# Down projection finished one token tile at a time, and a one-tensor form for the attention factors

## The chip, the core and the metric

The kernel runs on one core of a Trainium2 chip. The metric is device time in microseconds for one execution of the whole program, a two-layer transformer block over 1024 image tokens and 256 context tokens. The names of the engines: PE is TensorE (matmul; PEld is its weight load), DVE is VectorE, ACT is ScalarE, POOL is GpSimd, and SP issues most of the DMAs.

## The reference

Both layers are computed for `h` (1024 tokens of 1024 features); layer 0 also updates the context. What the change touches are the differential attention of layer 1 and the down projections of both feed-forward blocks:

```python
def diff_attention(q, k, v, lam):
    scale = DIFF_DH ** -0.5
    def blk(qb):
        s = jnp.einsum('bqhmd,bkhmd->bhmqk', qb, k).astype(jnp.float32) * scale
        p = jax.nn.softmax(s, axis=-1)
        w = (p[:, :, 0] - lam * p[:, :, 1]).astype(v.dtype)
        return jnp.einsum('bhqk,bkhe->bqhe', w, v)
...
def conv_ffn(u, w_up, conv_w, conv_b, w_down):
    a, g = jnp.split(u @ w_up, 2, axis=-1)
    g = dwconv(g, conv_w, conv_b, FFN_PAD)
    return (jax.nn.gelu(g) * a) @ w_down
...
h = h + ga2 * conv_ffn(u, ffn_w_up[li], ffn_conv_w[li], ffn_conv_b[li], ffn_w_down[li])
```

The hidden width is 2816 = 22 x 128. There are 8 heads, each with two maps (`m` = 0, 1) that are softmaxed apart and subtracted with the factor `lam`.

## The kernel before

**Products.** Every fp32 product is made of three matmuls on a high and a low part of each operand (`mm3`, lines 116, 117 and 118). A high part is a rounded copy (line 283 on ACT, line 90 on POOL), a low part is the difference of the value and its high part (line 98, on DVE or POOL).

**Down projection** (`ffn_down`). Layer 0 has three rounds of token tiles (0 to 3, 4 to 6, 7 to 9), layer 1 two (0 to 3, 4 to 7). A token tile is 128 tokens; its sum `acc` fills two PSUM banks, and a round of four tiles fills all eight. In a round the 22 weight tiles (`f`, 128 x 1024) go by in order, each with the matching piece of the hidden layer: an *item* of the list `items`. Step `i` issues the loads of item `i + 3` (SP), the split of item `i + 1` into high and low parts (ACT, then DVE), then item `i`'s matmuls for all tiles of the round, six for a tile. The split weights lie in rings of four buffers (`wh`, `wl`), the split hidden pieces in rings of three (`hh`, `hl`), the raw weights in a ring of three (`wr`). From round 1 of layer 0 on a step also takes one piece of `extra`, which prepares the finished tiles for layer 1 (square and scale, turn on PE, split).

After the 22 items each tile of the round is evacuated: DVE multiplies `acc` by a gain into `dtmp` (line 1244), POOL adds that to `ht` (line 1245), SP writes the sum out (line 1246). The very last tile is done in two halves, both operations on DVE. All of this stands in a written order: an engine takes its instructions in the order of the code.

**After layer 0's last round** comes `layer1_front`, whose order a scheduler makes. Its first weights `w_in_c` use the same rings `wr`, `wh` and `wl`; POOL makes the high part (line 90) and DVE the low part (line 98).

**Differential attention** (`diff_attn`). A head has four pairs of token tiles `a` and `b`, 32 pairs in all. `ORDER1` lists the operations of one step and by how many steps each lags. For DVE a step is, in this order: `m1a`, `m1b` (row maximum of map 1, line 1471), `ra` (reciprocal, line 1481), `ta` (the factor `tt` = first sum x -lam x reciprocal, line 1485), `pa` (the two maps combined, line 1487), `rb`, `m0b`, `m0a`, `tb`, `pb`. ACT makes the exponentials (line 1477) and copies of the turned maps (1499, 1506). POOL does `ha`, `la`, `hb`, `lb`: the high part of a turned map (line 90, `wh<-wf`) and its low part (line 98, `wl<-wf`). PE does the scores (1466), the turning (1492) and the product with `v` (1447).

Of the kernel before, what the change touches and what calls it, by code (L numbers as in the profile page):

```python
# [12 lines left out]
F32R = mybir.dt.float32r  # L13
# [5 lines left out]
P = 128  # L19
# [40 lines left out]
class K:  # L60
# [1108 lines left out]
    def ffn_down(self, l, rounds, dst, chunks, after):  # L1169

        nc, io = self.nc, self.io
        with ExitStack() as st:
            F = self.sb(st, f"down{l}")
            extra = []
            if after:
                Un = self.sb(after, "u1cols", side="right")
                self.u = {}
                AB = self.mod_finish(1, 0, 0)
            items = [(r, f) for r in range(len(rounds)) for f in range(NF)]
            raws, parts = {}, {}  # L1180

            def fetch(i):
                r, f = items[i]
                w = self.W.tile([P, 1024], F32, tag="wr", bufs=NWR, name="wr")
                nc.sync.dma_start(w, io["ffn_down"][l, f * P:(f + 1) * P, :])
                n = len(rounds[r]) * P
                x = F.tile([P, 512], F32, tag="hr", bufs=4, name="hr")[:, :n]
                nc.sync.dma_start(x, self.hid_d[f, :, rounds[r][0] * P:rounds[r][0] * P + n])
                raws[i] = w, x

            def split(i):
                w, x = raws.pop(i)
                n = x.shape[-1]
                hs = [F.tile([P, 512], F32R, tag="h" + y, bufs=3, name="h" + y)[:, :n] for y in "hl"]
                self.split(x, *hs)
                parts[i] = hs, self.split_new(w)

            def columns(t, ht):
                u = self.u[t] = [Un.tile([P, KT, P], F32R, tag=f"u{x}{t}", name="u") for x in "hl"]
                xn = F.tile([P, D], F32, tag="xn", bufs=2, name="xn")  # L1200
                v = F.tile([P, KT, P], F32, tag="v", bufs=2, name="v")
                return [lambda: self.scaled(F, ht, xn, xn.rearrange("p (k c) -> p k c", c=P)),
                        lambda: self.turned(xn, AB, v), lambda: self.split(v, *u)]

            with self.tc.manual_schedule():
                parts[0] = self.ahead
                for i in range(1, 3):
                    fetch(i)
                for r, tiles in enumerate(rounds):
                    with ExitStack() as s2:  # L1210
                        PS = self.PS = self.ps(s2, f"psD{l}{r}")
                        self.twos = 4 - len(tiles)
                        acc = {t: PS.tile([P, 2, 512], F32, tag="acc", bufs=len(tiles), name="acc") for t in tiles}
                        hts = {}
                        if r == 1:
                            extra = [step for ch in chunks for step in self.mod_steps(F, 1, ch, 1)] + extra
                        for f in range(NF):
                            i = r * NF + f
                            if i + 3 < len(items):
                                fetch(i + 3)  # L1220
                            if i == 4:
                                gas = [self.ga(F, l, 1, c, f"ga{c}") for c in range(2 if l == 0 else 1)]
                            if f == 8:
                                for t in tiles:
                                    hts[t] = F.tile([P, D], F32, tag="ht", bufs=8, name="ht")
                                    nc.sync.dma_start(hts[t], self.hm_d[t])
                            if i + 1 < len(items):
                                split(i + 1)
                            hs, w = parts.pop(i)
                            for j, t in enumerate(tiles):  # L1230
                                for b in range(2):
                                    self.mm3(acc[t][:, b, :], [x[:, j * P:(j + 1) * P] for x in hs],
                                             [x[:, b * 512:(b + 1) * 512] for x in w], f == 0, f == NF - 1)
                            if r:
                                coming = sum(3 * len(x) for x in rounds[r:-1]) if after else 0
                                for _ in range(-(-(len(extra) + coming) // (len(items) - i))):
                                    if extra:
                                        extra.pop(0)()
                        for t in tiles:
                            tmp = F.tile([P, D], F32, tag="dtmp", bufs=4, name="dtmp")  # L1240

                            last = l == 1 and t == NTX - 1
                            for c in [slice(0, 512), slice(512, D)] if last else [slice(0, D)]:
                                nc.vector.tensor_mul(tmp[:, c], acc[t].rearrange("p a b -> p (a b)")[:, c], gas[t >= NTX][:, c])  # L1244
                                (nc.vector if last else nc.gpsimd).tensor_tensor(hts[t][:, c], hts[t][:, c], tmp[:, c], op=ADD)  # L1245
                                nc.sync.dma_start(dst(t)[:, c], hts[t][:, c])
                        if after and r + 1 < len(rounds):
                            for t in tiles:
                                extra += columns(t, hts[t])
                assert not extra  # L1250
# [171 lines left out]
    def diff_attn(self):  # L1422
        nc, tc = self.nc, self.tc
        with ExitStack() as st:
# [12 lines left out]
            def emit(op, p):  # L1437
# [30 lines left out]
                elif op[0] == "m":  # L1468
                    m = int(op[1])
                    Y["m", m] = A.tile([P, 1], F32, tag=f"m{m}", bufs=4, name="m")  # L1470
                    nc.vector.tensor_reduce(Y["m", m], Y["S", m][:, :TOK], axis=AX.X, op=ALU.max, negate=True)  # L1471
                elif op[0] == "e":
                    m = int(op[1])
                    Y["p", m] = A.tile([P, TOK], F32, tag=f"p{m}", bufs=3 - m, name="p")
                    if m:
                        Y["s"] = A.tile([P, 1], F32, tag="s", bufs=4, name="s")
                    nc.scalar.activation(Y["p", m], Y["S", m][:, :TOK], AF.Exp, bias=Y["m", m],  # L1477
                                         accum_out=Y["s"] if m else s0[:, h, t:t + 1])
                elif op[0] == "r":
                    Y["r"] = A.tile([P, 1], F32, tag="r", bufs=4, name="r")  # L1480
                    nc.vector.reciprocal(Y["r"], Y["s"])
                elif op[0] == "t":

                    Y["tt"] = A.tile([P, 1], F32, tag="tt", bufs=4, name="tt")
                    nc.vector.scalar_tensor_tensor(Y["tt"], s0[:, h, t:t + 1], self.nlam, Y["r"], op0=MUL, op1=MUL)
                elif op[0] == "p":
                    nc.vector.scalar_tensor_tensor(Y["p", 0], Y["p", 1], Y["tt"], Y["p", 0], op0=MUL, op1=ADD)  # L1487
                elif op[0] == "T":
                    g = int(op[1])
                    Y["T", g] = PS.tile([P, 512], F32, tag="tp", bufs=2, name="tp")  # L1490
                    for k in range(min(4, NT - 4 * g)):
                        nc.tensor.transpose(Y["T", g][:, k * P:(k + 1) * P],
                                            Y["p", 0][:, (4 * g + k) * P:(4 * g + k + 1) * P], self.ident)
                elif op[0] == "f":
                    g = int(op[1])
                    n = min(4, NT - 4 * g)
                    if "wf" not in Y:
                        Y["wf"] = A.tile([P, NT, P], F32, tag="wf", bufs=2, name="wf")
                    nc.scalar.copy(Y["wf"][:, 4 * g:4 * g + n], Y["T", g][:, :n * P].rearrange("p (k c) -> p k c", c=P))
                elif op[0] == "h":  # L1500
                    if i == 0:
                        for w in ("wh", "wl"):
                            X[w] = A.tile([P, NT, 256], F32R, tag=w, bufs=2, name=w)
                    self.round_to("p", X["wh"][:, :8, c], Y["wf"][:, :8])
                elif op[0] == "x":
                    nc.scalar.copy(X["wh"][:, 8:, c], Y["wf"][:, 8:])  # L1506
                else:
                    self.rest("p", X["wl"][:, :, c], Y["wf"], X["wh"][:, :, c])
# [224 lines left out]
```

## Time and profile before

| what | value |
|---|---|
| median of 3 runs | 3381.88 us (3379.8 to 3381.99) |
| the profiled execution's own time | 3376.81 us |
| its span | 3375.0 us |
| mean granted TensorE clock | 0.982 |
| PE busy over the span | 94% |
| DVE busy over the span | 70% |
| POOL busy over the span | 28% |
| DMA read / written | 319.89 / 111.34 MB |

A duration in the profile holds what an instruction waits for once it has been started, so one and the same instruction can have several durations; the gap ahead of it is what it waited for before that, and the square bracket of a row says whose work ended that gap. Shares over the whole span hide that the stages have different limits.

### The profile page before, as it was taken

To read this page: it belongs to the slowest core of one execution; us is meant where nothing else is said; L and a number is where in the kernel's file an instruction comes from. 1 tells how busy PE (TensorE), PEld (TensorE's weight loads), DVE (VectorE), ACT (ScalarE), POOL (GpSimd) and SP (SyncE) were. 2 spreads that over 40 slices of the span, in tenths; PEclk is the share of its full clock that TensorE was granted. 3 is DMA by queue.
4 is the path that set the end of the run, shared out by engine and by line. 5 is a ranking of instruction groups with operands and counts; after the bars stand their busy time and mean duration, and the time that the engine had idled before them with its cause. 6 is when DMAs were issued, how large, how long until landed. Compare 5 with 4: busy or idle time off the path is not lost.

```text
span 3375.0 us, 43426 instructions
## 1 busy us (share of the span) xinstructions
PE 3161.4 (94%) x16262; PEld 2615.9 (78%) x16262; DVE 2368.7 (70%) x3381; ACT 1411.5 (42%) x2444; POOL 951.7 (28%) x654
## 2 busy tenths in 40 slices
PE   8998989989799999999999999888888899999998
PEld 4777778878688888877777777677877678888887
DVE  6478978864877777544556896699997787666443
ACT  3355766743433333323342121577763433333222
POOL 2223578864000000001113332377774200000010
PEclk9999999999999999999999999999999999999999
DMA  7223954334132232154555555534414123222553
GB/s 265 71 76 127 285 145 104 90 115 144 60 104 99 87 106 92 65 195 148 195 183 210 146 165 163 142 99 114 130 44 169 57 99 105 77 87 79 194 189 119
DMA packets 232298, 434.07 MB, mean 129 GB/s; under 512 B 21484, under 2 KB 147692, under 8 KB 230296
## 3 DMA queue, kind: packets, MB, share of 16 engines
q1 hardware_dynamic: 230216, 424.49, 39.8%
q10 hardware_dynamic: 1872, 6.82, 0.6%
q8 instruction: 128, 2.10, 0.3%
q14 instruction: 82, 0.67, 0.1%
HBM read 319.89 MB, written 111.34 MB: 128 GB/s over the span
## 4 chain that ended last, share of the span: by engine, by line
PE 56%; DVE 13%; issue 5%; ACT 2%; DMA 2%; POOL 1%; SPq 0%; DVEq 0%; ACTq 0%; POOLq 0%
PE pB L116 5%; PE pB L118 5%; PE pB L117 5%; PE acc L118 4%; PE acc L116 4%; PE acc L117 4%; DVE m L1471 3%; PE pj L116 3%; DVE p L1487 2%; PE pj L117 2%; PE pj L118 2%; PE pE L118 2%; PE pE L116 2%; PE pE L117 2%; PE S L1466 2%
## 5 line engine op out<-in xcount | busy, mean ns | idle before, releaser
L98 DVE TENSOR_TENSOR wl<-wr,wh 128x1024 fp32r<-128x1024 f32 (+2 forms) x287 | 350.8, 1231 | 100.0 <-ACT wh L283 70.6
L118 PE MATMUL acc<-wl,hh 128*128 128x512 f32 x776 | 304.8, 393 | 7.7 <-DVE wl L98 7.6
L116 PE MATMUL acc<-wh,hh 128*128 128x512 f32 x776 | 305.4, 394 | 5.8 <-ACT wh L283 5.8
L1245 POOL TENSOR_TENSOR ht<-ht,dtmp 128x1024 f32<-128x1024 f32 x17 | 44.7, 2660 | 919.2 <-DVE dtmp L1244 919.2
L117 PE MATMUL acc<-wh,hl 128*128 128x512 f32 x776 | 303.7, 391 | 0.0
L98 POOL TENSOR_TENSOR wl<-wf,wh 128x1280 fp32r<-128x1280 f32 x64 | 221.7, 3465 | 106.1 <-ACT wh L1506 103.6
L1466 PE MATMUL S<-k,q 128*128 128x512 f32 (+1 forms) x768 | 197.6, 382 | 56.9 <-ACT p L1477 55.5
L283 ACT CAST wh<-wr 128x1024 fp32r<-128x1024 f32 (+1 forms) x223 | 222.0, 1006 | 66.1 <-DVE wr L999 42.2
L98 DVE TENSOR_TENSOR hl<-hr,hh 128x512 fp32r<-128x512 f32 (+1 forms) x108 | 74.5, 690 | 224.8 <-ACT hh L283 224.7
L116 PE MATMUL pB<-ht,wh 128*128 128x512 f32 x528 | 210.0, 398 | 15.2 <-ACT ht L283 4.8
L118 PE MATMUL pB<-lt,wh 128*128 128x512 f32 x528 | 209.7, 397 | 3.0 <-DVE lt L98 2.9
L117 PE MATMUL pB<-ht,wl 128*128 128x512 f32 x528 | 209.3, 396 | 0.8 <-DVE wl L98 0.8
L116 PE MATMUL pj<-wh,u 128*128 128x512 f32 x448 | 180.7, 403 | 17.8 <-DVE qT L98 14.5
L1477 ACT ACTIVATE p<-S,m 128x1280 f32<-128x1280 f32 x128 | 170.9, 1335 | 61.5 <-DVE m L1471 58.2
L1471 DVE TENSOR_REDUCE m<-S 128x1 f32<-128x1280 f32 x128 | 187.1, 1480 | 8.4 <-PE S L1466 7.6
L1466 PEld LDWEIGHTS S<-k,q 128*128 128x128 f32 x768 | 124.7, 193 | 78.2 <-ACT p L1477 64.1
L283 ACT CAST hh<-hr 128x512 fp32r<-128x512 f32 (+1 forms) x108 | 62.5, 579 | 290.0 <-PE acc L118 258.7
L118 PEld LDWEIGHTS acc<-wl,hh 128*128 128x128 f32 x776 | 146.6, 189 | 43.1 <-DVE wl L98 12.8
L117 PE MATMUL pj<-wh,u 128*128 128x512 f32 x448 | 178.8, 399 | 0.0
L118 PE MATMUL pj<-wl,u 128*128 128x512 f32 x448 | 178.0, 398 | 0.0
L1037 ACT COPY g<-pB 128x512 f32<-128x512 f32 x84 | 49.6, 590 | 304.9 <-PE pB L118 304.9
L116 PEld LDWEIGHTS acc<-wh,hh 128*128 128x128 f32 x776 | 146.7, 189 | 38.8 <-ACT wh L283 9.1
(420 smaller groups left out, 9093.8 us busy)
## 6 DMA issues: line engine op xcount, KB each, us to landing
wr<-ffn_down SPq DMA_DIRECT2D x110, 512.0 KB
wr<-ffn_up SPq DMA_DIRECT2D x90, 512.0 KB
wr<-w_mod SPq DMA_DIRECT2D x76, 512.0 KB
hid<-gc SPq DMA_DIRECT2D x44, 512.0 KB
k<-dk SPq DMA_DIRECT2D x14, 1280.0 KB
hr<-hid SPq DMA_DIRECT2D x64, 256.0 KB
wr<-w_in_c SPq DMA_DIRECT2D x24, 512.0 KB
mr<-w_mod SPq DMA_DIRECT2D x20, 512.0 KB
```

Of the source, the lines that this page charges most:

```text
L98: e.tensor_tensor(out, x, hi.bitcast(F32), op=SUB)
L116: mm(out, a[0], b[0], start=start, stop=False, skip_group_check=onto)
L117: mm(out, a[1], b[0], start=False, stop=False, skip_group_check=onto)
L118: mm(out, a[0], b[1], start=False, stop=stop, skip_group_check=onto)
L283: self.nc.scalar.copy(hi, x)
L1037: nc.scalar.copy(out, x)
L1245: (nc.vector if last else nc.gpsimd).tensor_tensor(hts[t][:, c], hts[t][:, c], tmp[:, c], op=ADD)
L1466: nc.tensor.matmul(Y["S", m][:, c0:c0 + n], heads[h]["q"][m][:, t * P:(t + 1) * P], heads[h]["k"][x, m, j], start=(x == 0), stop=(x == 1))
L1471: nc.vector.tensor_reduce(Y["m", m], Y["S", m][:, :TOK], axis=AX.X, op=ALU.max, negate=True)
L1477: nc.scalar.activation(Y["p", m], Y["S", m][:, :TOK], AF.Exp, bias=Y["m", m], accum_out=Y["s"] if m else s0[:, h, t:t + 1])
L1487: nc.vector.scalar_tensor_tensor(Y["p", 0], Y["p", 1], Y["tt"], Y["p", 0], op0=MUL, op1=ADD)
```

## The change

In `ffn_down` the steps of a round's last three items still load and split, but issue no matmul. After the last step each tile of the round takes the matmuls of these three items (18 of them), and is evacuated behind them, before the next tile's 18 are issued. For this the rings `hh` and `hl` get a fourth buffer, the three items' parts are kept until the round's end, and the pieces of `extra` are spread over three steps fewer. In the attention the factor `tt` is computed by a `tensor_scalar` with one tensor operand and two per-partition factors; before it was a `scalar_tensor_tensor` with two tensor operands and one factor.

```diff
+            ends = 3
...
-                hs = [F.tile([P, 512], F32R, tag="h" + y, bufs=3, name="h" + y)[:, :n] for y in "hl"]
+                hs = [F.tile([P, 512], F32R, tag="h" + y, bufs=4, name="h" + y)[:, :n] for y in "hl"]
...
+            def product(out, i, j):
+                hs, w = parts[i]
+                f = items[i][1]
+                for b in range(2):
+                    self.mm3(out[:, b, :], [x[:, j * P:(j + 1) * P] for x in hs],
+                             [x[:, b * 512:(b + 1) * 512] for x in w], f == 0, f == NF - 1)
...
-                            hs, w = parts.pop(i)
+                            if f >= NF - ends:
+                                continue
                             for j, t in enumerate(tiles):
-                                for b in range(2):
-                                    self.mm3(acc[t][:, b, :], [x[:, j * P:(j + 1) * P] for x in hs],
-                                             [x[:, b * 512:(b + 1) * 512] for x in w], f == 0, f == NF - 1)
+                                product(acc[t], i, j)
+                            parts.pop(i)
                             if r:
...
-                                for _ in range(-(-(len(extra) + coming) // (len(items) - i))):
+                                for _ in range(-(-(len(extra) + coming) // max(1, len(items) - i - ends))):
...
-                        for t in tiles:
+                        for j, t in enumerate(tiles):
+                            for e in range(i - ends + 1, i + 1):
+                                product(acc[t], e, j)
                             tmp = F.tile([P, D], F32, tag="dtmp", bufs=4, name="dtmp")
...
+                        for e in range(i - ends + 1, i + 1):
+                            parts.pop(e)
...
-                    nc.vector.scalar_tensor_tensor(Y["tt"], s0[:, h, t:t + 1], self.nlam, Y["r"], op0=MUL, op1=MUL)
+                    nc.vector.tensor_scalar(Y["tt"], s0[:, h, t:t + 1], self.nlam, Y["r"], op0=MUL, op1=MUL)
```

On PE, in round 0 of layer 0, this is how the first of the last three items is left before the change; `acc_13462` and `acc_13463` are the sums of tiles 0 and 1, `wh_14134` and `wl_14135` that item's weights:

```order
L117 MATMUL acc_13462<-wh_14134,hl_14131 128x512
L118 MATMUL acc_13462<-wl_14135,hh_14130 128x512
L116 MATMUL acc_13463<-wh_14134,hh_14130 128x512
L117 MATMUL acc_13463<-wh_14134,hl_14131 128x512
L118 MATMUL acc_13463<-wl_14135,hh_14130 128x512
```

And at the same place now; `wh_14170` and `wl_14171` are the next item's weights:

```order
L117 MATMUL acc_13462<-wh_14134,hl_14131 128x512
L118 MATMUL acc_13462<-wl_14135,hh_14130 128x512
L116 MATMUL acc_13462<-wh_14170,hh_14166 128x512
L117 MATMUL acc_13462<-wh_14170,hl_14167 128x512
L118 MATMUL acc_13462<-wl_14171,hh_14166 128x512
```

Where PE went on to the next tile with the same weights, it now stays on the tile and goes on to the next weights; the number of matmuls is the same.

On POOL, at the end of layer 0's last round, before (`wh<-wr` is the high part of a `w_in_c` tile, `ht<-ht,dtmp` the evacuation's addition):

```order
L260 TENSOR_SCALAR xn<-ht,rs_y 128x1024
L90 TENSOR_SCALAR wh<-wr 128x1024 x3
L1245 TENSOR_TENSOR ht<-ht,dtmp 128x1024
L90 TENSOR_SCALAR wh<-wr 128x1024
L1245 TENSOR_TENSOR ht<-ht,dtmp 128x1024 x2
```

And now:

```order
L260 TENSOR_SCALAR xn<-ht,rs_y 128x1024
L90 TENSOR_SCALAR wh<-wr 128x1024
L1256 TENSOR_TENSOR ht<-ht,dtmp 128x1024
L90 TENSOR_SCALAR wh<-wr 128x1024
L1256 TENSOR_TENSOR ht<-ht,dtmp 128x1024
L90 TENSOR_SCALAR wh<-wr 128x1024 x2
L1256 TENSOR_TENSOR ht<-ht,dtmp 128x1024
```

The roundings of the new stage's weights moved in between the additions. In the attention no row changes its place on any engine; on DVE the row of `tt` changes its kind, from `SCALAR_TENSOR_TENSOR` to `TENSOR_SCALAR`.

## Rows read from the trace of the kernel before

**Rows 1.** Two stretches: us; busy of PE, PEld, DVE, ACT, POOL; clock; DMA; GB/s

```profile
2143.00:2538.00 395.00, 339.85 (x2258) 300.91 (x2258) 379.29 (x322) 292.81 (x530) 279.81 (x126) 0.98 0.39 105
...
3129.00:3366.00 237.00, 235.91 (x1038) 194.71 (x1038) 93.82 (x92) 64.78 (x82) 14.20 (x6) 1.00 0.47 161
```

**Rows 2.** The factor `tt` by tile: duration in ns, least, median, greatest

```profile
L1485 DVE SCALAR_TENSOR_TENSOR tt<-s,nlam,r x64: 210/724/1501, 2143.2 to 2535.8; 128x1 f32<-128x1 f32 x64
```

**Rows 3.** The same, grouped over the attention: busy us, mean ns

```profile
L1485 DVE SCALAR_TENSOR_TENSOR tt<-s,nlam,r 128x1 f32<-128x1 f32 x64 | 66.1, 1033 | 3.3 <-ACT p L1477 1.5
```

**Rows 4.** Timeline of DVE over one pair: start, us, instruction

```profile
2298.79 2.88 DVE L1471 TENSOR_REDUCE m<-S 128x1 f32<-128x1280 f32 x2
...
2301.95 0.70 DVE L1485 SCALAR_TENSOR_TENSOR tt<-s,nlam,r 128x1 f32<-128x1 f32 x1
2302.69 1.55 DVE L1487 SCALAR_TENSOR_TENSOR p<-p,tt 128x1280 f32<-128x1280 f32 x1
...
2307.25 1.49 DVE L1485 SCALAR_TENSOR_TENSOR tt<-s,nlam,r 128x1 f32<-128x1 f32 x1
2308.77 2.30 DVE L1487 SCALAR_TENSOR_TENSOR p<-p,tt 128x1280 f32<-128x1280 f32 x1
2311.00 1.48 DVE L1471 TENSOR_REDUCE m<-S 128x1 f32<-128x1280 f32 x1
```

**Rows 5.** Timeline of POOL beside it

```profile
2301.60 1.05 POOL L90 TENSOR_SCALAR wh<-wf 128x1024 fp32r<-128x1024 f32 x1
2305.77 2.95 POOL L98 TENSOR_TENSOR wl<-wf,wh 128x1280 fp32r<-128x1280 f32 x1 [3.12 <-ACT wh L1506]
2308.69 1.04 POOL L90 TENSOR_SCALAR wh<-wf 128x1024 fp32r<-128x1024 f32 x1
2309.82 4.04 POOL L98 TENSOR_TENSOR wl<-wf,wh 128x1280 fp32r<-128x1280 f32 x1
```

**Rows 6.** Timeline of ACT, the pair's first exponential

```profile
2300.30 1.33 ACT L1477 ACTIVATE p<-S,m 128x1280 f32<-128x1280 f32 x1 [1.51 <-DVE m L1471]
```

**Rows 7.** A 128x1 instruction with one tensor operand, by line

```profile
L258 DVE TENSOR_SCALAR ss<-ss x38: 140/152/156, 6.6 to 2673.9; 128x1 f32<-128x1 f32 x38
```

**Rows 8.** Timeline of DVE at the end of layer 0's round 0

```profile
1563.29 5.30 DVE L1244 TENSOR_TENSOR dtmp<-acc,ga 128x1024 f32<-128x1024 f32 x4 [4.07 <-PE acc L118]
1568.51 1.28 DVE L98 TENSOR_TENSOR hl<-hr,hh 128x384 fp32r<-128x384 f32 x1
1569.72 3.40 DVE L98 TENSOR_TENSOR wl<-wr,wh 128x1024 fp32r<-128x1024 f32 x1
1573.04 0.14 DVE L258 TENSOR_SCALAR ss<-ss 128x1 f32<-128x1 f32 x1
```

**Rows 9.** Timeline of POOL beside it

```profile
1564.60 10.77 POOL L1245 TENSOR_TENSOR ht<-ht,dtmp 128x1024 f32<-128x1024 f32 x4 [286.50 <-DVE dtmp L1244]
```

**Rows 10.** Timeline of PE behind it

```profile
1573.17 0.50 PE L118 MATMUL acc<-wl,hh 128*128 128x512 f32 x1 [1.31 <-DVE wl L98]
...
1579.22 0.98 PE L270 MATMUL ntp<-ident,xn 128*128 128x128 f32 x7 [2.12 <-POOL xn L260]
```

**Rows 11.** The page's group of the low parts made on DVE

```profile
L98 DVE TENSOR_TENSOR wl<-wr,wh 128x1024 fp32r<-128x1024 f32 (+2 forms) x287 | 350.8, 1231 | 100.0 <-ACT wh L283 70.6
```

**Rows 12.** Timeline of PE behind layer 0's round 1

```profile
1677.32 0.51 PE L118 MATMUL acc<-wl,hh 128*128 128x512 f32 x1 [2.63 <-DVE wl L98]
```

**Rows 13.** Busy time and granted clock just behind it, columns as in rows 1

```profile
1677.00:1681.00 4.00, 3.68 (x9) 2.90 (x10) 2.58 (x8) 0.00 (x0) 2.62 (x2) 0.58 1.00 322
```

**Rows 14.** Timeline of DVE at the program's end

```profile
3361.41 4.77 DVE L1244 TENSOR_TENSOR dtmp<-acc,ga 128x1024 f32<-128x1024 f32 x4 [9.48 <-PE acc L118]
3366.21 1.76 DVE L1245 TENSOR_TENSOR ht<-ht,dtmp 128x512 f32<-128x512 f32 x1
...
3368.61 2.11 DVE L1245 TENSOR_TENSOR ht<-ht,dtmp 128x512 f32<-128x512 f32 x1
```

**Rows 15.** Timeline of POOL beside it

```profile
3362.71 7.46 POOL L1245 TENSOR_TENSOR ht<-ht,dtmp 128x1024 f32<-128x1024 f32 x3 [109.25 <-DVE dtmp L1244]
```

## The prediction

> **What bounds the kernel now.** I read the table of stretches first, since the page's 94% for PE is a mean over stages with different limits. In layer 1's down projection (3129 to 3366) PE is busy 235.91 of 237 us; in the attention (2143 to 2538) it is busy 339.85 of 395 while DVE is busy 379.29, that is 96% [rows 1]. So the attention is DVE's stage, and the down projections are PE's except at the ends of their rounds. In DVE's stage one group stands out: `tt`, one element per partition, has 64 instructions that together take 66.1 us, 1033 ns each [rows 3], though the quickest needs 210 ns [rows 2].
>
> The timelines of DVE and POOL laid side by side say why [rows 4, 5]. The first `tt` of the pair ends at 2302.65, and so does POOL's `wh` (2301.60 + 1.05). The second runs from 2307.25 to 2308.74; POOL's `wl` ends at 2308.72. The `p` behind it starts at 2308.77, while POOL's next `wh` runs to 2309.73, and ends 1.34 us after that, at 2311.07; the other `p`, with nothing beside it, takes 1.55. POOL suffers in turn: its second `wl` takes 4.04, and 2311.07 to its end at 2313.86 is 2.79. So a DVE instruction with two SBUF tensors and a POOL instruction exclude each other for a whole instruction, and where POOL has its next one ready, the DVE instruction that already waits goes first. The first goes for `hl` and `wl` behind a round as well: `wl` takes 3.40 beside POOL's additions [rows 8, 9] and 1.23 on average [rows 11]. An instruction with one tensor operand of 128x1 is not shut out: at 1573.04 one takes 0.14 in the middle of an addition [rows 8, 9], and none of 38 takes over 156 ns [rows 7].
>
> **The attention, step by step.** The new `tt` has one tensor operand of 128x1. Its two factors come by partition, which rows 7 don't show; its cost lies between 0.14 and the 1033 of now, and I take 0.2, nearest to rows 7 and to the quickest old one. That alone doesn't give 0.83 us back 64 times, because `p` right behind it has two SBUF tensors and meets the same POOL instruction. So I replay a pair.
>
> - First `tt`: it ends at about 2302.15 in place of 2302.65, but `p` then waits for POOL's `wh` to 2302.65 and ends 1.34 later at 2303.99, against 2304.24. That moves `m` of map 0, behind it, up by 0.25, and the second `tt`, but not POOL's `wl` beside that, which starts on ACT's release [rows 5]. Gain at the pair's end: 0.
> - Second `tt`: it is done by about 2307.5, and `p` waits for `wl` to end at 2308.72. It has then been waiting in the place that `tt` held, so it goes ahead of POOL's `wh`: 2308.72 + 1.34 = 2310.06, against 2311.07. Gain: 1.01.
> - What is late next: POOL's `wh` starts at 2310.06 and ends at 2311.10, its `wl` (2.95) at 2314.05. The next pair's `m` now starts 1.01 earlier, at 2309.99, so `wl` ends 4.06 into that pair, later than the 2.81 of now (2301.60 - 2298.79). The first `p`, asking at 3.4, waits for that and ends at 5.40; today it ends at 5.45. Nothing behind it moves.
>
> The pair shrinks from 12.21 us (2311.00 - 2298.79) to 11.20. The loop that then sets it is `m`, ACT's exponential, which starts on it [rows 6], ACT's copies, POOL's `wl`, which starts on them [rows 5], `p`, and `m`. PE needs 339.85/395 of 12.34 (a 32nd of the stretch), 10.6 us, so it still fits. How many pairs gain: 32 first factors of about 0.71 are 22.7 of the 66.1 us, and the 43.4 left are 29 of 1.49. Term: 29 x 1.01 = 29.3 us.
>
> The Trainium skill weighs in here. Its page "SBUF — State Buffer", section "SBUF: two separate sides", says that VectorE and GpSimd share a port pair as an exclusive lock for a whole instruction, and that VectorE needs it with two SBUF inputs or in a two-port performance mode. The page "VectorE: DVE Perf Modes", section "Mode 2×_2P — use both read ports for one tensor", gives that mode to fp32 `tensor_scalar`. Rows 4 and 5 agree with the lock. By the mode the new `tt` would be shut out like the old one and the term would be 0; the 0.14 at 1573.04 speaks against that for a single element per partition. It is the third rival below.
>
> **The ends of the rounds.** The matmul count is unchanged. PE issues one per 0.227 us (235.91/1038 [rows 1]), so a tile's 18 take 4.09 and a tile's six 1.36: before, the tiles of a round end 1.36 apart, now 4.09 apart. An addition on POOL takes 2.69 (10.77/4 [rows 9]), a multiplication on DVE about 1.3 (5.30/4 [rows 8]). Before, POOL fell behind and its additions covered the next split on DVE; now all but the last are over when PE leaves the round (T).
>
> - Behind the last tile: the multiplication ends at T + 1.4; the next item's `hl` (0.5) either slips in ahead of the addition or waits for it; `wl` ends at the latest 1.2 behind the addition, T + 1.4 + 0.5 + 2.5 + 1.1, about T + 5.5, and without any collision at T + 3.1. The new order adds one wait: this split needs buffers that three held items free only in the last tile, at T - 2.7, which is before DVE can take it.
> - Rounds 0 to 1 and 1 to 2 of layer 0: the next item lasts 18 x 0.227 = 4.1, so `wl` is wanted at about T + 4.4: a wait of 0 to 1.1, I take 1.1, since the collision is what rows 8 show. Before, 1.31 and, for the turning behind POOL's queue, 2.12 [rows 10]; the second goes, as POOL's additions are over. Gain 3.4 - 1.1 = 2.3, at most 3.4. At the second place 2.63 [rows 12], and behind it the clock fell to 0.58, between its levels of 1.2 and 2.4 GHz [rows 13], which costs 0.42 x 4 = 1.7. A wait of 1.1 is less than half of 2.63, and I let it cost no clock. Gain 4.3 - 1.1 = 3.2, at most 4.3.
> - Layer 1's round 0 has four tiles in the next item (5.4 us): covered, 0; without that cover 0.8.
> - Into `layer1_front`: three of four weight buffers are held to T - 2.7, T - 1.4 and T, so POOL's roundings stand between the additions. POOL: rounding to T - 1.7, addition to T + 1.0, two roundings to T + 3.1, addition to T + 5.8. DVE's low parts queue behind these, and the last ends at about T + 8. Loss between 0 and 1.5; I take 0.7.
> - The program's end: the last two DVE additions took 1.76 and 2.11 beside POOL's additions, which ran to 3370.17 [rows 14, 15]. Now POOL is done by T + 0.1. Nearest row for a free 128x512 addition: 0.14 + half of 1.23, about 0.7. So 1.06 + 1.41 = 2.5 earlier; the last write has fewer bytes in front of it, 0 to 1. I take 2.9.
>
> Sum: 2.3 + 3.2 - 0.7 + 2.9 = 7.7.
>
> The fourth buffer of `hh` and `hl` adds no instruction; what hides it is that a split already ran two items ahead of PE, and in layer 1's rounds PE waited for none (1.1 us of idle in 237 [rows 1]).
>
> **Total.** 29.3 + 7.7 = 37. The profiled execution took 3376.8, so 3339.8. The median of the runs, 3381.9, is 5.1 above it; on that footing I forecast 3345.
>
> **Rivals.**
>
> 1. The wait only moves to `p`: at the end of POOL's `wl` its next instruction gets in first. For it: the second `p` lost just so, to a `wh` that had already started. Against: both times DVE was waiting at an end, it won, with the second `tt` at 2308.74 and `p` at 2309.73. Then the attention gains 0, total -7.7: 3374.
> 2. More than forecast: ACT's copies come earlier in the shorter pair and PE becomes the bound. Its 10.6 with some of its present waits left, say the middle between that and 11.2, is 10.9, so 29 x 1.3 = 38; with the upper ends of the other terms (3.4 + 4.3 + 0 + 3.5 = 11.2) -49: 3333. For it: POOL still has slack. Against: `wl` follows ACT, and ACT follows `m`.
> 3. The change doesn't do what it says: the new `tt` is shut out as well. Attention 0, 3374.
> 4. Slower: the next split is shut out twice, `hl` by the last addition and `wl` by POOL's next instruction, so that `wl` comes at T + 6.6. At three ends PE then idles 2.2 and runs on at the slow clock (1.7): 3 x 3.9 = 11.7 against 7.7 now (3.4 + 4.3), and 0.9 in layer 1: +4.9, and with nothing from the attention 3387. It decides from the point at which POOL has a second instruction ready when the addition ends. Against: rows 8 show `hl` in between two additions.
>
> **How the numbers follow.** Forecast 0.70, with its own range of 3336 to 3354 (pairs 0.85 to 1.1 each, ends 5 to 11). Rival 1 has 0.13, rival 2 0.07, rival 3 0.06, rival 4 0.04. A measurement of this kernel tells about 0.2% from no change, 6.8 us. Forecast and rival 2 are faster by more, rivals 1 and 3 (7.7 us, 0.23%) in about half of the cases: 0.77 + 0.10 = 0.87 faster; the other half and most of rival 4 within, 0.11; slower 0.02. The range takes in rival 2 down to 3330, and rivals 1 and 3 up to 3374.
>
> **What would show it.** In the new profile: all `tt` at about 0.2; both `p` of a pair above 1.55, the second ending 1.3 after POOL's `wl`; `m` to `m` 11.2; POOL's second `wl` back to 2.95; DVE idle ahead of neither. At the round ends no wait of PE over 1.3 and no clock below full; the two last additions 0.7 each. I am wrong if `tt` still follows POOL's ends, if the second `p` ends behind POOL's `wh`, or if the pair stays at 12.2.

## The result and the profile after

The changed kernel takes 3339.66 us in the median of four runs (3337.66 to 3341.32); beside it the kernel before took 3380.84 (3379.58 to 3381.99). The ratio is 0.9878, with an interval of [0.9861, 0.9895], so it is 41 us faster, between 35 and 47. The forecast was 3345, with a range of 3330 to 3374. The profiled execution took 3341.32 with a span of 3339.5, which is 35.5 less than the span of before. Where these 35.5 lie is read by taking the same matmul in both traces and subtracting its start:

| stretch | forecast | read from the two traces |
|---|---|---|
| start, up to layer 0's down projection | 0 | 2.5 longer |
| layer 0, end of round 0 | -2.3 | -2.7 |
| layer 0, end of round 1 | -3.2 | -3.4 |
| last round's end and `layer1_front` | +0.7 | -1.2 |
| attention and what follows it, up to layer 1's feed-forward block | -29.3 | -26.4 |
| layer 1, end of round 0 | 0 | -0.4 |
| the program's end | -2.9 | -3.9 |

The 2.5 at the start lies in code that the change doesn't touch, almost all of it within the first 45 us. At 45 us the twelve other kernels profiled in this study are 1.5 to 3.0 us later than the one profiled execution of before as well, so it is that execution which was early there. At the start of the down projection they are 0.1 to 7.0 later, so a row of one trace on code that is the same may be off by some us. Without the 2.5 the sum is 38.0, against a forecast of 37.

In the table of stretches, the attention of the new profile is the first line (us; busy us and count of PE, PEld, DVE, ACT, POOL; clock; DMA share; GB/s); the second is the 4 us behind layer 0's round 1, which answer to [rows 13]:

```profile
2138.20:2507.10 368.90, 340.80 (x2264) 302.29 (x2265) 347.66 (x322) 293.39 (x531) 320.87 (x127) 0.97 0.42 112
1673.50:1677.50 4.00, 3.42 (x16) 2.50 (x15) 3.23 (x8) 0.00 (x0) 1.81 (x3) 1.00 0.69 219
```

PE's busy time in the attention is within 1 us of what it was [rows 1], in a stretch that is 26 us shorter; DVE is still busy for 94% of it. The clock behind the round is now 1.00, where it had been 0.58 [rows 13].

By tile and by group (as [rows 2, 3]), `tt` and the `p` behind it:

```profile
L1498 DVE TENSOR_SCALAR tt<-s,nlam,r x64: 268/274/278, 2138.4 to 2503.7; 128x1 f32<-128x1 f32 x64
L1500 DVE SCALAR_TENSOR_TENSOR p<-p,tt 128x1280 f32<-128x1280 f32 x64 | 138.2, 2160 | 2.2
L1498 DVE TENSOR_SCALAR tt<-s,nlam,r 128x1 f32<-128x1 f32 x64 | 17.5, 274 | 3.5 <-ACT p L1490 1.5
```

None of the 64 is shut out any more: 59 of them lie wholly inside a POOL instruction, and the slowest takes 278 ns. They gave up 66.1 - 17.5 = 48.6 us of DVE's busy time. Some 15 of these came back in `p`, whose mean rose from 1929 to 2160 ns. That is the wait which the prediction moved from `tt` to `p`. Timelines of DVE and of POOL over one pair (as [rows 4, 5]):

```profile
2291.34 0.27 DVE L1498 TENSOR_SCALAR tt<-s,nlam,r 128x1 f32<-128x1 f32 x1
2291.65 2.51 DVE L1500 SCALAR_TENSOR_TENSOR p<-p,tt 128x1280 f32<-128x1280 f32 x1
2294.09 2.88 DVE L1484 TENSOR_REDUCE m<-S 128x1 f32<-128x1280 f32 x2
...
2297.26 0.27 DVE L1498 TENSOR_SCALAR tt<-s,nlam,r 128x1 f32<-128x1 f32 x1
2297.57 1.90 DVE L1500 SCALAR_TENSOR_TENSOR p<-p,tt 128x1280 f32<-128x1280 f32 x1
```

```profile
2289.87 2.95 POOL L98 TENSOR_TENSOR wl<-wf,wh 128x1280 fp32r<-128x1280 f32 x1 [0.71 <-ACT wh L1519]
2292.79 2.28 POOL L90 TENSOR_SCALAR wh<-wf 128x1024 fp32r<-128x1024 f32 x1
2295.16 2.95 POOL L98 TENSOR_TENSOR wl<-wf,wh 128x1280 fp32r<-128x1280 f32 x1
2298.07 2.30 POOL L90 TENSOR_SCALAR wh<-wf 128x1024 fp32r<-128x1024 f32 x1
```

The second `p` (2291.65) waits until POOL's `wl` ends at 2292.82, and ends 1.34 us after that, at 2294.16. POOL's next instruction, `wh`, was started at 2292.79 but takes 2.28 in place of 1.04: it was the one that had to wait. So DVE's waiting instruction got the turn, twice in a pair, and POOL pays in `wh` what it paid before in its second `wl` (4.04 then, 2.95 now). From one second `p` to the next the pair takes 11.2 us. In the whole attention 58 of the 64 `p` end in this way, 1.3 us behind a `wl`.

At the end of layer 0's round 0, DVE, POOL and PE (as [rows 8, 9, 10]):

```profile
1569.90 1.23 DVE L1255 TENSOR_TENSOR dtmp<-acc,ga 128x1024 f32<-128x1024 f32 x1 [2.85 <-PE acc L118]
1571.04 0.55 DVE L98 TENSOR_TENSOR hl<-hr,hh 128x384 fp32r<-128x384 f32 x1
1571.50 3.42 DVE L98 TENSOR_TENSOR wl<-wr,wh 128x1024 fp32r<-128x1024 f32 x1
```

```profile
1571.20 2.63 POOL L1256 TENSOR_TENSOR ht<-ht,dtmp 128x1024 f32<-128x1024 f32 x1 [1.67 <-DVE dtmp L1255]
```

```profile
1574.97 0.50 PE L118 MATMUL acc<-wl,hh 128*128 128x512 f32 x1 [0.58 <-DVE ss L258]
```

PE leaves the round at T, just ahead of the last multiplication at 1569.90. `hl` slips in ahead of POOL's last addition, `wl` is shut out until that ends at 1573.83, and is done at T + 5.0. PE waits 0.58, and there is no second wait for the turning; the end of round 1 is the same to 0.1 us. At the program's end both halves' additions on DVE now take 0.69 (as [rows 14]):

```profile
3334.65 0.69 DVE L1256 TENSOR_TENSOR ht<-ht,dtmp 128x512 f32<-128x512 f32 x1
...
3335.98 0.69 DVE L1256 TENSOR_TENSOR ht<-ht,dtmp 128x512 f32<-128x512 f32 x1
```

### The profile page after: what moved, and what is told of

Its sections match the earlier page's. It is cut to its first block, busy times and chain, and to the rows that moved or that the text cites. A ratio compares the mean times of both kernels' runs of the same rounds, so it can differ in the third digit from the quotient of the medians.

```text
span 3339.5 us, 43491 instructions
## 1 busy us (share of the span) xinstructions
PE 3163.0 (95%) x16262; PEld 2617.9 (78%) x16262; DVE 2330.3 (70%) x3381; ACT 1411.1 (42%) x2444; POOL 988.6 (30%) x654
## 4 chain that ended last, share of the span: by engine, by line
PE 59%; DVE 11%; ACT 3%; issue 2%; DMA 2%; POOL 1%; SPq 0%; ACTq 0%; DVEq 0%; POOLq 0%
PE acc L118 5%; PE acc L116 5%; PE acc L117 5%; PE pB L116 5%; PE pB L118 5%; PE pB L117 5%; PE S L1479 3%; DVE m L1484 2%; PE pj L116 2%; DVE p L1500 2%; PE pE L118 2%; PE pE L116 2%; PE pE L117 2%; PE pj L117 2%; PE pj L118 2%
## 5 line engine op out<-in xcount | busy, mean ns | idle before, releaser
L90 POOL TENSOR_SCALAR wh<-wf 128x1280 fp32r<-128x1280 f32 (+1 forms) x128 | 221.1, 1730 | 82.5 <-ACT wf L1512 66.9
L98 POOL TENSOR_TENSOR wl<-wf,wh 128x1280 fp32r<-128x1280 f32 x64 | 189.8, 2966 | 38.2 <-ACT wh L1519 31.2
L116 PE MATMUL pj<-wh,u 128*128 128x512 f32 x448 | 180.2, 403 | 15.7 <-DVE qT L98 14.0
```

Source lines behind the costliest of these rows:

```text
L90: nc.gpsimd.tensor_scalar(out, x, 1.0, 1.0, op0=MUL, op1=MUL)
L98: e.tensor_tensor(out, x, hi.bitcast(F32), op=SUB)
L116: mm(out, a[0], b[0], start=start, stop=False, skip_group_check=onto)
```

## The experiments

Each ratio is to the kernel before, timed beside it in five rounds.

| kernel | median, us | ratio | a pair, us |
|---|---|---|---|
| new `tt` alone | 3352.75 | 0.9922 [0.9908, 0.9935] | 11.2 |
| down projection alone | 3364.65 | 0.9955 [0.9941, 0.9969] | 12.2 |
| new `tt` for the second tile of a pair only | 3337.40 | 0.9874 [0.9861, 0.9887] | 11.2 |
| new `tt` for the first tile only | 3365.40 | 0.9956 [0.9943, 0.9968] | 12.2 |
| `tt` two elements wide | 3372.71 | 0.9977 [0.9967, 0.9986] | 12.2 |
| two weight tiles kept for a round's end | 3343.73 | 0.9893 [0.9878, 0.9908] | 11.2 |
| one weight tile kept | 3354.28 | 0.9923 [0.9910, 0.9937] | 11.2 |
| three kept in layer 0's last round only | 3348.77 | 0.9903 [0.9890, 0.9917] | 11.2 |
| POOL's `wl` in 768 and 512 columns | 3327.37 | 0.9845 [0.9832, 0.9859] | 10.6 to 11.0 |
| ... and the additions in halves | 3328.04 | 0.9841 [0.9828, 0.9855] | 10.6 to 11.0 |
| `wl` in 640 and 640 columns | 3323.10 | 0.9831 [0.9818, 0.9844] | 10.7 to 11.0 |
| ... with the old `tt` | 3367.13 | 0.9964 [0.9951, 0.9978] | 11.0 to 13.8 |

**The two edits apart.** The kernel before with the new `tt`, and the changed kernel with the old one:

```
- nc.vector.scalar_tensor_tensor(Y["tt"], s0[:, h, t:t + 1], self.nlam, Y["r"], op0=MUL, op1=MUL)
+ nc.vector.tensor_scalar(Y["tt"], s0[:, h, t:t + 1], self.nlam, Y["r"], op0=MUL, op1=MUL)
```

> The kernel before with the new form of the factor tt in the attention, and the old end of the down projection's rounds. Theory (the two edits add up, each in its own stage): pairs of the attention at 11.2 us in place of 12.2, some 26 to 29 us less over the stage, nothing elsewhere; the ratio to the kernel before is 0.992 (about 3353 to 3356). Rival (the two lean on each other, or part of the gain comes from work that starts earlier): below 0.990 or above 0.995.

> The changed kernel with the old form of tt: the down projection's change alone. Theory: waits of PE at the ends of layer 0's rounds of 0.58 each, about 3 us less at either, 2.5 to 4 less at the program's end, pairs of the attention at 12.2; together 8 to 11 us, ratio 0.997. Rival (nothing of it reaches the end of the program, the attention's gain is the whole): 0.999 or more.

The first came out as expected: 27.6 us less. The second is 15.7 us less (10 to 20 by its interval), and 8 to 11 were expected. 27.6 + 15.7 = 43.3, and together they gave 41.2, so they add up within their uncertainty. The down projection's share was forecast too small, 7.7: the table above has 11.6 for it, with the difference in `layer1_front` and at the program's end. The rest of the 15.7 is not explained. In the trace of the second kernel 5 us of its gain lie between the attention and layer 1's down projection, in code that the change does not touch.

**Which of the two `tt` counts.** Only one of the two tiles gets the new form:

```
+ if i == 1:      # i == 0 in the other kernel
+     nc.vector.tensor_scalar(Y["tt"], ...)
+ else:
+     nc.vector.scalar_tensor_tensor(Y["tt"], ...)
```

> The changed kernel with the new form of tt for the second token tile of a pair only, the old one for the first. Theory (only the second one's place in front of the rounding on POOL counts): pairs stay at 11.2, as long as the changed kernel within 2 us, ratio 0.988; the first tt is shut out for about 0.5 and the first p then needs no wait. Rival (each tt gives back what it waited, a third of it at the first): about 9 us slower than the changed kernel, ratio 0.9905.

> The changed kernel with the new form of tt for the first token tile of a pair only. Theory: pairs stay at 12.2, the attention gains nothing, ratio 0.996 to 0.997 (the down projection alone). Rival (each gives back what it waited): pairs at about 11.8, ratio 0.992 to 0.993.

Theory and rival lie 9 to 12 us apart, and the measurement decides for the replay: the second alone gives everything (3337.40, pairs 11.2), the first alone nothing beyond the down projection (3365.40 against 3364.65, pairs 12.2). DVE with the new form for the second only, in one pair:

```profile
2292.97 0.27 DVE L1499 TENSOR_SCALAR tt<-s,nlam,r 128x1 f32<-128x1 f32 x1
2293.27 1.62 DVE L1503 SCALAR_TENSOR_TENSOR p<-p,tt 128x1280 f32<-128x1280 f32 x1
...
2297.97 0.88 DVE L1501 SCALAR_TENSOR_TENSOR tt<-s,nlam,r 128x1 f32<-128x1 f32 x1
2298.89 2.30 DVE L1503 SCALAR_TENSOR_TENSOR p<-p,tt 128x1280 f32<-128x1280 f32 x1
```

One detail of the expectation failed: the first `p` was to need no wait, and takes 2.30, as it lost its turn to a rounding just as the second one did before. The pair is 11.2 all the same, so this wait had room behind it.

**How wide may the free form be.** `tt` for two elements a partition, of which one is used:

```
- nc.vector.tensor_scalar(Y["tt"], s0[:, h, t:t + 1], self.nlam, Y["r"], op0=MUL, op1=MUL)
+ nc.vector.tensor_scalar(Y["tt"], self.nlam2, s0[:, h, t:t + 1], Y["r"], op0=MUL, op1=MUL)  # 128x2
```

> The changed kernel, but tt is made for two elements a partition in place of one: the tensor operand is a 128x2 tile that holds -lambda twice, the factors are the first sum and the reciprocal, and only the first column is used. Theory (a single element per partition is what lets the one-tensor form past POOL; a wider one needs the same lock as two tensors): the second tt takes about 1.5 again, pairs 12.2, ratio 0.9955 as with the down projection alone (about 3365). Rival (any short instruction with one tensor operand goes past POOL): tt at 0.27, pairs 11.2, ratio 0.988.

By tile:

```profile
L1501 DVE TENSOR_SCALAR tt<-nlam,s,r x64: 280/750/1509, 2143.0 to 2534.7; 128x2 f32<-128x2 f32 x64
```

The quickest takes 280 ns, as the one-element form does, and the median 750, with the old pattern of 0.7 and 1.5 in turn; 60 of the 64 end together with a POOL instruction. So the theory holds for one element against two. Wider operands were not run, nor one element with the operands in the places that they have here. The attention has lost all of its gain. The total is 8.1 us above the down projection alone, more than the edit explains; in the traces 3.4 of that lie ahead of layer 1, and why stays open. The Trainium skill, page "VectorE: DVE Perf Modes", section "Mode 2×_2P — use both read ports for one tensor", gives fp32 `tensor_scalar` the two-port mode on a condition: the outermost dimension longer than one has to be even, or odd and equal in source and result. The runs agree: two elements meet the condition and were shut out, while one element has no dimension longer than one, and all 59 that lay inside a POOL instruction took 268 to 278 ns.

**How many weight tiles a round has to keep.**

```
- ends = 3
+ ends = 2        # and 1 in the other kernel
```

> The changed kernel with two weight tiles kept for the end of a round in place of three, so that tiles of a round end 2.72 us apart in place of 4.08. Theory (what counts is that POOL's additions, 2.4 to 2.7 each, keep up with the tiles): waits of 0.6 at the ends of layer 0's rounds and the same tail, as long as the changed kernel within 3 us, ratio 0.988. Rival (the spacing itself counts, each item kept gives a share): half of the down projection's gain is lost, about 7 us slower, ratio 0.990.

> The changed kernel with one weight tile kept for the end of a round, which leaves TensorE the old order at the ends: of the down projection's change only the fourth buffer and the spreading of the preparing work over one step fewer stay. Theory (the gain there is the order's): as the new tt alone, 3353, ratio 0.992. Rival (the fourth buffer lets splits run further ahead): below 0.990.

With one, TensorE's order at the ends is that of before; 3354.28 is the time of the new `tt` alone (3352.75) within the runs' spread. The fourth buffer and the other spreading of the preparing work are worth nothing that these runs can tell. With two, the ends of layer 0's rounds come within 0.1 us of those with three, and the program's end within 0.2: tiles 2.72 apart are enough for additions of 2.4. The 2 us more in its trace (4 in the medians) arise in `layer1_front`, where PE waits 4.87 at one place some 30 us into the stage, less what is given back later:

```profile
1802.33 0.77 PE L116 MATMUL pj<-wh,u 128*128 128x512 f32 x1 [4.87 <-DVE vst L98]
```

So the theory holds for the ends of the rounds, and the total lies between the two expectations.

**Where `layer1_front` gained.** Three weight tiles kept in layer 0's last round, one in all others:

```
- ends = 3
+ ends = 3 if l == 0 and r == last_round else 1
```

> The changed kernel with three weight tiles kept for the end of layer 0's last round only, one in all the other rounds, which leaves these in the old order. Theory (the last round's new end costs about 0.9 at the next stage's first weights and gives back 2 to 4 later, where the turning of its tiles no longer waits for POOL's additions): 1 to 3 us less than with one everywhere (3354), ratio 0.9915 to 0.992; in the trace a wait of about 0.5 at the first weights, and under 2 us of waits in place of 3.35 in the next 40 us. Rival (the later gain came from the earlier rounds, or from a DMA that lands at another time): the waits of 0.90 and 2.45 are there as in the kernel before.

In layer 0 the pieces of `extra` are spread as in the changed kernel, so this kernel differs from the one with one tile kept in that too. PE's waits over the stage's first 40 us: of the kernel before, of the one with one tile kept, of the changed kernel, and of this one:

```profile
1801.99 0.47 PE L116 MATMUL pj<-wh,u 128*128 128x512 f32 x1 [0.90 <-DVE vst L98]
1811.15 0.79 PE L116 MATMUL pj<-wh,u 128*128 128x512 f32 x1 [2.45 <-ACT v L275]
```

```profile
1803.50 0.47 PE L116 MATMUL pj<-wh,u 128*128 128x512 f32 x1 [0.16 <-DVE vst L98]
1812.67 0.80 PE L116 MATMUL pj<-wh,u 128*128 128x512 f32 x1 [2.46 <-DVE vst L98]
```

```profile
1775.85 0.50 PE L118 MATMUL pj<-wl,u 128*128 128x512 f32 x1 [0.49 <-DVE wl L98]
1806.61 0.47 PE L116 MATMUL pj<-wh,u 128*128 128x512 f32 x1 [1.74 <-DVE vst L98]
```

```profile
1786.44 0.50 PE L118 MATMUL pj<-wl,u 128*128 128x512 f32 x1 [0.49 <-DVE wl L98]
```

The last round's new end costs 0.9 us over the first 15 us (a wait of 0.49 is what shows), and the waits 15 to 40 us later shrink or go. The clock is as large a part of it. Behind the wait of 2.45 it fell to 0.60 in the kernel before, where the first matmul took 0.79; behind the 1.74 of the changed kernel it stays at 1.00. In both, the 4 us that begin just ahead of the end of that wait (columns as in [rows 1]):

```profile
1810.00:1814.00 4.00, 2.85 (x7) 2.28 (x8) 4.00 (x4) 2.14 (x4) 2.31 (x2) 0.60 0.59 224
```

```profile
1806.00:1810.00 4.00, 3.40 (x15) 2.78 (x16) 3.96 (x4) 2.15 (x4) 2.30 (x2) 1.00 0.79 297
```

Between 1800 and 1815 the changed kernel gains 3.3 us on the one before: 0.9 and 0.7 are waits, and the 1.6 left is about what the slow clock costs (0.40 of 4 us). Over the whole stage this kernel is 3.0 us shorter than the one with one tile kept; the medians differ by 5.5. So this stage's gain comes from this round. How is open. That it is the norms of the last tiles, which start earlier because POOL's additions are over, fits the rows of POOL: its first `rs_y` of the stage follows the last multiplication by 10.3 us in the changed kernel and 11.1 in this one, in place of 13.0. But with two tiles kept it follows by 10.8 and PE waits 4.87 all the same. There ACT's copy of `vst` is held for 12.23 us by a DMA, where it was 7.0 in the kernel before and in the changed one, so the rival of a DMA that lands at another time is not out:

```profile
1799.75 0.59 ACT L283 CAST vst<-pj 128x512 fp32r<-128x512 f32 x1 [12.23 <-DMA dv<-vst]
```

**A better kernel: shorter instructions on POOL.** If what `p` waits for is a whole POOL instruction, shorter ones must help:

```
- self.rest("p", X["wl"][:, :, c], Y["wf"], X["wh"][:, :, c])
+ for k in (slice(0, 6), slice(6, NT)):      # (0, 5), (5, NT) in the other kernel
+     self.rest("p", X["wl"][:, k, c], Y["wf"][:, k], X["wh"][:, k, c])
```

> The changed kernel, with POOL's low part of a turned map (2.95 us, 1280 columns) made in two instructions of 768 and 512 columns. Theory (the second p still waits 1.17 for POOL's low part to end, and goes in at the next boundary): the second p at 1.6 to 1.9, pairs at 10.7 to 11.0, 6 to 15 us less than the changed kernel, ratio 0.983 to 0.986. Rival (the pair is bound by POOL's own chain, which gets two instructions more): pairs at 11.2 to 11.4, ratio 0.988 to 0.990.

> The kernel with POOL's low part in two instructions, now of 640 columns each in place of 768 and 512. Theory (a boundary anywhere near the middle is enough; TensorE's 10.6 sets the pair): pairs at 10.6 to 11.0, ratio 0.983 to 0.986, within 3 us of the other cut. Rival (the boundary has to fall where the second p asks): pairs at 11.2, ratio 0.988.

Both gave the forecast pair, 10.8 to 10.9 us, and the forecast ratio. Two details failed: with 768 and 512 the second `p` takes 1.8 to 2.2 in most pairs, not 1.6 to 1.9, and the two cuts lie 4.3 us apart, not within 3, though their intervals overlap. With equal halves it is the fastest kernel of the study, 3323.10, 16.6 us under the changed one. DVE and POOL there:

```profile
2283.53 2.15 DVE L1500 SCALAR_TENSOR_TENSOR p<-p,tt 128x1280 f32<-128x1280 f32 x1
...
2288.94 2.04 DVE L1500 SCALAR_TENSOR_TENSOR p<-p,tt 128x1280 f32<-128x1280 f32 x1
```

```profile
2284.43 4.19 POOL L98 TENSOR_TENSOR wl<-wf,wh 128x640 fp32r<-128x640 f32 x2
2288.59 1.05 POOL L90 TENSOR_SCALAR wh<-wf 128x1024 fp32r<-128x1024 f32 x1
```

Not for the reason given, though. In the changed kernel 58 of the 64 `p` wait for POOL's `wl`. Here one `p` of the first pairs goes in between two halves, and from then on 58 of the 64 arrive while POOL rounds: the first `p` above (2283.53) ends 1.3 behind a `wh`, and so does the second, 1.34 behind the `wh` of 2288.59 to 2289.64. A rounding is 1.04 long, so that both `p` wait 0.5 to 0.6, where in the changed kernel they waited 0.35 and 1.0. The halves of `wl` then wait together for one `p`, 4.19 in place of 2.95.

This order is not needed for the gain either. With 768 and 512 columns ten pairs in the second half of the stage run in the order of the changed kernel, with both pieces of `wl` back to back, each `p` behind them and `wh` held for 2.3, and still take 10.7 to 10.9:

```profile
2349.72 2.28 POOL L90 TENSOR_SCALAR wh<-wf 128x1024 fp32r<-128x1024 f32 x1
2352.08 3.11 POOL L98 TENSOR_TENSOR wl<-wf,wh 128x768 fp32r<-128x768 f32 x2
```

What these pairs have in common shows on PE. One pair of the changed kernel, one with equal halves and one of those ten (columns as in [rows 1]):

```profile
2286.36:2297.57 11.21, 10.85 (x76) 9.69 (x75) 10.88 (x11) 9.36 (x18) 10.42 (x5) 1.00 0.05 13
```

```profile
2272.77:2283.53 10.76, 10.76 (x76) 9.67 (x75) 10.49 (x11) 9.30 (x18) 10.39 (x7) 1.00 0.05 14
```

```profile
2343.63:2354.49 10.86, 10.85 (x76) 9.68 (x75) 10.64 (x11) 9.30 (x18) 10.69 (x7) 1.00 0.77 169
```

A pair's 76 matmuls keep PE busy for 10.8, a little more than the 10.6 of the prediction. In these pairs PE idles for 0.00 and 0.01 with the cut, and for 0.36 without it, waiting for ACT's exponential:

```profile
2297.07 1.20 PE L1479 MATMUL S<-k,q 128*128 128x512 f32 x4 [0.36 <-ACT p L1490]
```

So with the cut PE is what bounds the pair. Why the cut takes away PE's last wait is not shown. Whether a whole `wl` would keep the shorter pair, once in it, was not tried.

**The same cut at the ends of the rounds.**

```
- nc.gpsimd.tensor_tensor(hts[t][:, c], hts[t][:, c], tmp[:, c], op=ADD)
+ for d in (slice(0, 512), slice(512, D)):
+     nc.gpsimd.tensor_tensor(hts[t][:, d], hts[t][:, d], tmp[:, d], op=ADD)
```

> The kernel with POOL's low part in two instructions of 768 and 512 columns, and now POOL's additions at the ends of the down projection's rounds in two halves of 512 columns as well. Theory (the low part of the next weights waits for a whole addition of 2.4; with halves it goes in after the first): TensorE's waits of 0.58 at the ends of layer 0's rounds go, the low part takes 2.2 to 2.5 in place of 3.4, 1 to 3 us in all, which the times can hardly tell from the kernel with the first cut alone (ratio 0.984). Rival (at the boundary POOL's second half goes in first): the low part still takes 3.4 and the waits stay at 0.58.

DVE, POOL and PE at the end of round 0:

```profile
1572.60 2.31 DVE L98 TENSOR_TENSOR wl<-wr,wh 128x1024 fp32r<-128x1024 f32 x1
```

```profile
1572.30 3.76 POOL L1257 TENSOR_TENSOR ht<-ht,dtmp 128x512 f32<-128x512 f32 x2 [1.53 <-DVE dtmp L1255]
1576.02 0.56 POOL L126 TENSOR_TENSOR rs_y<-ss,mhalf 128x1 f32<-128x1 f32 x1
1577.55 2.32 POOL L260 TENSOR_SCALAR xn<-ht,rs_y 128x1024 f32<-128x1024 f32 x1 [0.97 <-DVE rs_y L133]
```

```profile
1579.92 1.09 PE L270 MATMUL ntp<-ident,xn 128*128 128x128 f32 x8 [0.81 <-POOL xn L260]
```

The mechanism was right and the gain failed. `wl` takes 2.31 in place of 3.42 and PE's 0.58 is gone; but the second half of the addition is late by as much, the factor `rs_y` of the next tile to be turned stands behind it on POOL, `xn` needs that factor, and PE waits 0.81 for `xn`. The wait has changed its place: in the traces the ends of rounds 0 and 1 gain 0.1 to 0.2 us each on the kernel with the first cut alone. The totals agree with that (3328.04 against 3327.37), though the two traces differ by more elsewhere: `layer1_front` is 7.7 longer in this one, and why is not shown.

**Does the cut need the new `tt`?** The equal halves with the old form of `tt`:

> The kernel with POOL's low part in two instructions of 640 columns, but with the old form of tt, with two tensor operands. Theory (tt takes DVE's turn at POOL's next boundary, and p behind it then loses a turn to the second half or to the rounding): tt up to 1.2, p at 2.3 to 2.8, pairs at 11.2 to 11.8, ratio 0.988 to 0.992, so that the form of tt is still worth some 15 to 25 us. Rival (short pieces on POOL make every collision short, and the form of tt then hardly matters): pairs at 10.8 to 11.0, ratio 0.983 to 0.985.

```profile
2291.85 0.28 DVE L1498 SCALAR_TENSOR_TENSOR tt<-s,nlam,r 128x1 f32<-128x1 f32 x1
2292.17 2.96 DVE L1500 SCALAR_TENSOR_TENSOR p<-p,tt 128x1280 f32<-128x1280 f32 x1
```

```profile
2291.08 1.05 POOL L90 TENSOR_SCALAR wh<-wf 128x1024 fp32r<-128x1024 f32 x1
2292.21 1.57 POOL L98 TENSOR_TENSOR wl<-wf,wh 128x640 fp32r<-128x640 f32 x1
```

It does, and more than the theory said: 44 us separate the two forms of `tt` (3367.13 and 3323.10), where 15 to 25 were expected. The reason that it gave shows: `tt` takes the turn at 2292.13 (1.05 behind 2291.08), POOL's half of `wl` gets in ahead of `p`, and `p` needs 2.96. By its start `p` (2292.17) was even 0.04 ahead of that half (2292.21), and lost: it came up only after the end of `wh` at 2292.13. So it goes for 29 of the 40 long `p` of this kernel that wait for a half of `wl`. The price that the theory put on this was too small, since a pair now varies between 11.0 and 13.8: the stage takes 391.0 from its first `p` to the first `p` of its last pair, against 343.5 with the new form. With the old `tt` the cut is worth nothing (3364.65 without it).

## Why the prediction was right, step by step

- *`tt` goes past POOL.* Right, at 0.27 in place of my 0.2; the test with two elements shows how narrow the ground was on which this stood: a tile twice as wide would have lost the whole term. Nor did [rows 7] say as much as I read from them: in the trace of before only two of those 38 instructions lie inside a POOL instruction, the one at 1573.04 and one other; the other 36 met nothing.
- *First `tt` 0, second 1.01 a pair.* Right in both numbers: 12.21 to 11.20, and the test with one tile at a time gives the whole to the second. The first `p` was to be 2.00 long and is 1.90; the second was to wait 1.2 and end 1.34 later, and is 2.51 long.
- *29 pairs.* A little too many: the trace has 26.4 us in place of 29.3. Between the starts of their first `p`, the pair that also splits the weights of `w_out_c` takes 20.6 in place of 19.95, and does so in four other kernels with the new `tt` too; the first pair took 11.71 in place of 10.65, but varies between 9.8 and 11.7 over the kernels here. These two are 1.7 of the 2.9 that are missing.
- *Ends of the rounds.* 2.7 and 3.4 against 2.3 and 3.2. `wl` came at T + 5.0, not T + 5.5, and PE waits 0.58, not 1.1.
- *`layer1_front`.* This term failed. The entry's loss was there (0.9 against 0.7). What I had not followed was the other end: PE's waits of 0.90 and 2.45 some 30 us on, and the slow clock behind the second, hung on the round's end as well. By which chain is open. It came out as a gain of 1.2 in the profile of the changed kernel, 3.0 in the pair of kernels that isolates it.
- *The program's end.* 3.9 against 2.9. The additions gave 2.5, as worked out; the last write took 2.9 us from DVE's last instruction to the end of the span (3336.67 to 3339.5), against 4.3 before (3370.72 to 3375.0). So this was worth 1.4, beyond the end that I gave. It is no chance of one trace: the three other kernels that end layer 1 in the old order have 4.3 too, those with the new one 2.9 to 3.0. That fewer bytes stand ahead of the write fits, but was not tested by itself.
- *Rivals.* Rival 1 fell: POOL's next instruction did not get in first, as 58 of the 64 `p` went in right behind a `wl`; what moved from `tt` to `p` is 15 of 48.6 us, which the replay had counted. Rival 2 did not come: the pair stayed at 11.2, where PE still waits 0.36 a pair. In the kernels with `wl` cut its mechanism came: PE is the bound there, with 10.8. Rivals 3 and 4 fell: no `tt` is shut out, and no end of a round is slower. Rival 3 gave the new `tt` the two-port mode without looking at its condition, which a single element does not meet.

The sum came out right in part by luck. The attention gave 2.9 less than its term, while the front and the program's end gave 1.9 and 1.0 more, which is the same amount; the rest, 38.0 against 37, is the ends of the rounds. The forecast of 3345 is 5 above the median. Of these, 1 is that sum and 1 is that the kernel before took 3380.84 beside the changed one, not 3381.9. The other 3 come from where the two profiled executions lie among their runs: that of the changed kernel 1.7 above its median, that of before, without its early start, 1.5 under.

## What to carry to other kernels

Where two engines shut each other out for whole instructions, a tiny instruction can cost a full turn twice, by its own wait and by the turn that the large one behind it then loses; replay the order of turns before counting its busy time as the gain. Give the tiny one a form that needs no turn, and try to cut the other engine's long instructions; here the second paid only after the first, and then until PE had no wait left. And at the end of a stage, follow the freed engine's queue into the next stage, since a wait 30 us later may have its cause there.

## What the runs showed that was not expected

- One-tensor `TENSOR_SCALAR` on DVE beside POOL: with 128x1 at most 278 ns in 64 instructions, 59 of them wholly inside a POOL instruction; with 128x2 up to 1509.
- At a boundary between two POOL instructions the DVE instruction that already waits goes first, even where POOL's next one has already started by the profile: POOL's `wh` then takes 2.28 to 2.30, against 1.04. A `p` that came up only 0.04 us behind the boundary lost, though its start stands ahead of POOL's.
- The same pair has more than one stable rhythm: 11.2 us with a whole `wl`, 10.6 to 11.0 with a cut one, in two different orders, though POOL's work and DVE's are the same; with the old `tt` the halves made it irregular, 11.0 to 13.8.
